# Seven block products for the gate, up and first feed-forward matrices of a four-layer model

## The chip, the cores and the metric

The kernel runs on one core of a Trainium2 chip. The metric is the device time of one execution in microseconds; lower is better. Data lie in SBUF (128 partitions); TensorE multiplies into PSUM banks, VectorE, ScalarE and GpSimd work on the rest, and the DMA queues of SyncE bring the weights from HBM. In the profile they are PE (with PEld for its weight loads), DVE, ACT, POOL and SP.

## The reference, cut to what matters

512 tokens of width 1024 go through four layers, in float32. The first two end in a gated feed-forward block of inner width 2816, the last two in a squared-ReLU block of inner width 4096.

```python
def swiglu(h, wg, wu, wd):
    return (jax.nn.silu(h @ wg) * (h @ wu)) @ wd

def sq_relu_mlp(x, w_up, w_down):
    return jnp.square(jax.nn.relu(x @ w_up)) @ w_down

# first block, layers 0 and 1
    h = h + mix                      # hybrid mixer, then convolution
    h = h + swiglu(rms_norm(h, ffn_norm[layer]), wg, wu, wd)
# second block, layers 0 and 1
    x = x + rmsnorm(m, norm_mixer_post[i])      # m: attention, then short convolution
    h = rmsnorm(x, norm_mlp_pre[i])
    x = x + rmsnorm(sq_relu_mlp(h, mlp_w_up[i], mlp_w_down[i]), norm_mlp_post[i])
```

## The kernel before, in words

**Layout.** Activations are kept transposed: eight tiles `res[0..7]` of 128 channels x 512 tokens hold the residual in float32. A normalised copy lies in `xh` (high part, fp32r) and `xl` (the rest, fp32r). Scratch tiles of 128x512 come from two lists, `rslots` (fp32r) and `fslots` (float32), oldest first.

**Matrix products.** Each weight block is loaded as float32 (`wraw`, 2048 columns, three buffers) and split by `load_w` (L218) in two halves of 1024: ScalarE rounds to `wh` (the helper's line is L101 for everything that ScalarE does), VectorE subtracts to `wl` (L235); `wh` and `wl` have two buffers of 2048 each. `mm3` (L239) then makes three matmuls for each output tile and k, `wh*xh` (L240), `wh*xl` (L241) and `wl*xh` (L242), each 128x128 by 512 tokens. `group` (L246) does this for four outputs of 128 rows and eight k: two loads of four k, 96 matmuls, four PSUM banks, after which `evac` takes each output. The tag `mm` has four banks and `at` four.

**Norms.** Only the gain is put in before a product (`split_x`, L332: ScalarE writes `xh`, VectorE `xl` at L334). The tokens' scale `rb` is made beside it by `bc_rstd`: `sumsq` squares the eight residual tiles on ScalarE, sums five on GpSimd (L316) and three on VectorE, and two matmuls with a matrix of ones (L326) give the sum over the channels to all partitions. `rb` is then multiplied into each output when it is taken.

**The gated block** `swiglu` (L606) has three parts of 8, 8 and 6 row tiles. A group computes two gate tiles and two up tiles: gate tiles are scaled (L621), put through SiLU on ScalarE and scaled again on GpSimd (L623), up tiles are multiplied by them (L625) and split (L339) to `hh`, `hl`. After each part `out_proj` multiplies by the second matrix and adds to the residual.

**The other block** `mlp` has four parts of two groups of four tiles each. `evac` scales (L1010), squares the ReLU (L1011) and splits (L339). The second matrix's outputs are added up in `post.m`; class `Post` squares and sums them (L791, GpSimd adds), makes their scale for each half of 256 tokens (L818), and `apply` multiplies (L810), adds to the residual (L811) and splits for the next product. The first groups of a block take their first load in halves of 256 tokens (`halves`), so that they can begin on the first half.

**What sets the order.** The program is written in the order of the data; the framework's scheduler puts every engine's instructions in a fixed row, and each engine works in that order. Tiles in the lists and pools come free when their last reader is done.

## Time and profile before

| | |
|---|---|
| time, median of 3 runs | 2519.17 us (2518.61 to 2525.0) |
| the profiled execution | 2523.11 us |
| its span in the trace | 2521.1 us |
| mean granted TensorE clock, share of full speed | 0.982 |
| PE busy, share of the span | 97% |
| DVE busy | 49% |
| ACT busy | 36% |
| POOL busy | 10% |
| read from HBM | 202.61 MB |

A matmul's end is modelled, so that a busy time adds up overlaps; the distance from one start to the next is what one costs in a row of them. A timeline row gives the start in us, its length, engine, line, operation, output and inputs, shape and count; a bracket behind it gives the engine's idle time ahead of the row and what ended it. A count above 1 joins equal neighbours.

### The profile page before, as it was taken

Reading aid. Unit: us, or ns where it says so; the run is one execution under the profiler, and the core shown is the slowest. Engines: PE = TensorE matmul, PEld = TensorE weight load, DVE = VectorE, ACT = ScalarE, POOL = GpSimd, SP = SyncE. Lnnn points to the kernel's source line nnn. Section 1 sums busy time; section 2 is a strip of 40 time slices with the busy share of each in tenths; the row PEclk is TensorE's granted clock in tenths of the full one; section 3 lists DMA queues with packets and bytes.
Section 4 is the critical chain, followed back from the end, with each engine's and each line's share of the span. In section 5 each row is a group of like instructions: output and inputs, shape, how many; then the busy total and the mean of one; then the engine's idle time right before and its main releaser. Section 6 shows DMA issues by size and latency. Waiting matters only on the chain.

```text
span 2521.1 us, 26712 instructions
## 1 busy us (share of the span) xinstructions
PE 2447.7 (97%) x10910; PEld 1940.4 (77%) x10910; DVE 1236.3 (49%) x1674; ACT 900.6 (36%) x1546; POOL 242.7 (10%) x223
## 2 busy tenths in 40 slices
PE   8999999999998799999999998999998999999997
PEld 6677788888786578888887677788887887788886
DVE  4333543333599744333345765443446544533454
ACT  4663432222664333222244455322224224322222
POOL 0000010100103111010100004000004103000002
PEclk9999999999999899999999999999999999999998
DMA  5112222322311132232232112233232222222320
GB/s 171 34 51 77 74 93 91 100 86 91 97 46 55 33 97 94 91 100 86 82 101 67 53 49 68 85 100 100 84 100 67 93 92 84 84 89 95 101 84 34
DMA packets 148075, 206.42 MB, mean 82 GB/s; under 512 B 5822, under 2 KB 88305, under 8 KB 147953
## 3 DMA queue, kind: packets, MB, share of 16 engines
q1 hardware_dynamic: 147921, 204.72, 25.3%
q8 instruction: 85, 1.39, 0.2%
q14 instruction: 37, 0.30, 0.0%
q10 hardware_dynamic: 32, 0.01, 0.0%
HBM read 202.61 MB, written 2.10 MB: 81 GB/s over the span
## 4 chain that ended last, share of the span: by engine, by line
PE 61%; DVE 3%; POOL 2%; ACT 2%; issue 1%; ACTq 0%; POOLq 0%; DVEq 0%
PE ps L242 18%; PE ps L240 18%; PE ps L241 18%; DVE fs L717 1%; ACT fs L101 1%; PE ps L912 1%; POOL fs L811 1%; PE ps L948 1%; POOL fs L316 1%; PE ps L285 1%; PE ps L284 1%; PE ps L283 1%; DVE fs L810 0%; POOL fs L791 0%; PE ps L940 0%
## 5 line engine op out<-in xcount | busy, mean ns | idle before, releaser
L240 PE MATMUL ps<-rs,wh 128*128 128x512 f32 (+1 forms) x3008 | 1176.2, 391 | 12.7 <-ACT rs L101 8.9
L241 PE MATMUL ps<-rs,wh 128*128 128x512 f32 (+1 forms) x3008 | 1173.2, 390 | 4.0 <-DVE rs L334 4.0
L242 PE MATMUL ps<-rs,wl 128*128 128x512 f32 (+1 forms) x3008 | 1171.7, 390 | 2.4 <-DVE wl L235 2.4
L235 DVE TENSOR_TENSOR wl<-wraw,wh 128x1024 fp32r<-128x1024 f32 (+2 forms) x386 | 459.5, 1219 | 711.7 <-ACT wh L101 706.9
L101 ACT ACTIVATE wh<-wraw 128x1024 fp32r<-128x1024 f32 (+2 forms) x386 | 385.3, 1039 | 890.3 <-PE ps L241 612.7
L240 PEld LDWEIGHTS ps<-rs,wh 128*128 128x128 f32 x3008 | 570.1, 190 | 146.6 <-ACT rs L101 11.3
L241 PEld LDWEIGHTS ps<-rs,wh 128*128 128x128 f32 x3008 | 570.8, 190 | 136.0 <-DVE rs L334 5.4
L242 PEld LDWEIGHTS ps<-rs,wl 128*128 128x128 f32 x3008 | 570.3, 190 | 131.0 <-DVE wl L235 2.9
L101 ACT ACTIVATE fs<-fs 128x512 f32<-128x512 f32 (+2 forms) x289 | 154.4, 549 | 174.6 <-DVE fs L621 93.7
L101 ACT ACTIVATE rs<-fs 128x512 fp32r<-128x512 f32 x160 | 97.6, 616 | 189.6 <-DVE fs L1011 112.2
L339 DVE TENSOR_TENSOR rs<-fs,rs 128x512 fp32r<-128x512 f32 x136 | 93.8, 696 | 51.1 <-ACT rs L101 51.0
L791 POOL TENSOR_TENSOR fs<-fs,fs 128x256 f32<-128x256 f32 (+1 forms) x44 | 46.1, 1047 | 753.6 <-ACT fs L101 752.7
L623 POOL TENSOR_TENSOR fs<-fs,fs 128x512 f32<-128x512 f32 x44 | 56.6, 1288 | 621.1 <-ACT fs L101 594.3
L717 DVE SCALAR_TENSOR_TENSOR fs<-fs,vec,fs 128x497 f32<-128x497 f32 (+15 forms) x139 | 98.0, 778 | 0.0
L101 ACT ACTIVATE fs<-ps 128x512 f32<-128x512 f32 (+1 forms) x99 | 50.8, 524 | 69.2 <-PE ps L242 30.7
L706 PE MATMUL ps<-rs,rs 128*128 128x500 f32 (+13 forms) x279 | 67.8, 397 | 7.9 <-ACT rs L101 7.9
L316 POOL TENSOR_TENSOR fs<-fs,fs 128x512 f32<-128x512 f32 x28 | 46.9, 1676 | 278.8 <-ACT fs L101 277.7
L706 PEld LDWEIGHTS ps<-rs,rs 128*128 128x128 f32 x279 | 53.8, 193 | 21.2 <-ACT rs L101 9.8
L101 ACT ACTIVATE rs<-fs,vec 128x512 fp32r<-128x512 f32 (+1 forms) x76 | 48.2, 651 | 60.5 <-DVE fs L811 15.9
L334 DVE SCALAR_TENSOR_TENSOR rs<-fs,vec,rs 128x512 fp32r<-128x512 f32 (+1 forms) x76 | 60.4, 829 | 7.3 <-ACT rs L101 7.1
L283 PE MATMUL ps<-wh,rs 128*128 128x512 f32 (+1 forms) x160 | 62.2, 391 | 0.0
L284 PE MATMUL ps<-wl,rs 128*128 128x512 f32 (+1 forms) x160 | 61.9, 387 | 0.0
(201 smaller groups left out, 1456.9 us busy)
## 6 DMA issues: line engine op xcount, KB each, us to landing
wraw<-in_mlp_w_up_dram SPq DMA_DIRECT2D x32, 1024.0 KB
wraw<-in_mlp_w_down_dram SPq DMA_DIRECT2D x32, 1024.0 KB
wraw<-in_ffn_w_gate_dram SPq DMA_DIRECT2D x44, 512.0 KB
wraw<-in_ffn_w_up_dram SPq DMA_DIRECT2D x44, 512.0 KB
wraw<-in_ffn_w_down_dram SPq DMA_DIRECT2D x20, 1024.0 KB
wraw<-in_cv_w_pw_dram SPq DMA_DIRECT2D x16, 512.0 KB
wraw<-in_attn_w_qkv_dram SPq DMA_DIRECT2D x16, 512.0 KB
wraw<-in_conv_w_in_dram SPq DMA_DIRECT2D x16, 512.0 KB
```

The source lines that it names most:

```text
L101: r = self.engine.activation(out, in_, func, **kw)
L235: dve.tensor_sub(wl[:, s], raw[:, s], b(wh[:, s]))
L240: pe.matmul(ps, wh, h, start=start, stop=False, skip_group_check=True)
L241: pe.matmul(ps, wh, l, start=False, stop=False, skip_group_check=True)
L242: pe.matmul(ps, wl, h, start=False, stop=stop, skip_group_check=True)
L283: pe.matmul(ps, hs[kk + k][:, ts_], wh[:, k, :], start=ci == 0 and k == 0, stop=False)
L284: pe.matmul(ps, hs[kk + k][:, ts_], wl[:, k, :], start=False, stop=False)
L316: r = eng.tensor_add(acc, acc, s)
L334: dve.scalar_tensor_tensor(xl[k][:, x], res[k][:, x], gain, b(xh[k][:, x]), ALU.mult, ALU.subtract)
L339: dve.tensor_sub(l, src, b(h))
L706: pe.matmul(pc[:, s:], d, x[:, : T - s], start=i == 0, stop=i == len(todo) - 1, skip_group_check=True)
L717: dve.scalar_tensor_tensor(x[:, s:], u[:, : T - s], wdv(s, ct), x[:, s:], ALU.mult, ALU.add)
```

## The change

Both first matrices are multiplied in quarters. For a group of four row tiles, the weights (1024 channels x 512 rows) and the normalised tokens (1024 channels x 512 tokens) are cut into 2x2 blocks, and the four output blocks (256 rows x 256 tokens) are made of seven block products instead of eight (the Winograd form of Strassen's scheme). Each product is 4 k x 2 row tiles x 3 = 24 matmuls with 256 tokens, into one PSUM bank.

- `group_s` replaces `group`. It loads the weights into the same two `wraw` buffers, makes sums of weight blocks in place on VectorE, splits seven 1024-wide parts (`w_parts`: four buffers each of `wh` and `wl`, 1024 wide), and adds the products up on VectorE. `evac(n, th, ps)` gets row-tile pair `n` and token half `th`, two row tiles beside each other.
- The sums of token blocks are made once for a block, when the residual is ready: `xh`, `xl` of channels 0 to 511 hold the first half of the tokens and a difference of the halves; three further combinations lie in `so[0]` (high) and `so[1]` (rest). `split_s` and `split_s_half` take the place of `split_x` there.
- In `swiglu` the up tiles come first: they keep no scale; the gate tiles are scaled and put through SiLU; the tokens' scale of the up tiles is multiplied in after the second matrix (`down_evac`). GpSimd's L623 goes. In `mlp` nothing is scaled behind the first matrix; ScalarE does ReLU and square; `rb` squared is multiplied in after the second (`evac_last`).
- Constants, the stage of the vectors, five float tiles and the rounded constants move to pools that live for one phase (`Phase`), so that `so` finds room.

```diff
-NF = 34
+NF = 29
+NX = 5
...
-    rslots = [cpool.tile([P, T], F32R, name=f"rs{i}") for i in range(32)]
+    pairs = [cpool.tile([P, 2, T], F32R, name=f"rs{i}") for i in range(16)]
+    rslots = [p[:, h, :] for p in pairs for h in range(2)]
...
+    def w_parts(src, n):
+        wh = wpool.tile([P, 1024], F32R, tag="wh", name=f"wh{n_p[0]}", bufs=4)
+        wl = wpool.tile([P, 1024], F32R, tag="wl", name=f"wl{n_p[0]}", bufs=4)
...
+        act.activation(v(wh), src, AF.Copy)
+        dve.tensor_sub(v(wl), src, v(b(wh)))
+        return wh, wl
...
-        wh = wpool.tile([P, 2048], F32R, tag="wh", name=f"wh{i}", bufs=2)
-        wl = wpool.tile([P, 2048], F32R, tag="wl", name=f"wl{i}", bufs=2)
...
+    def open_s():
+        ph = Phase(0)
+        for i in range(2):
+            so[i] = ph.tile([P, 4, 3, 256], F32R, f"so{i}")
+        return ph
+
+    def split_s3(k, gain):
+        d = F()
+        dve.tensor_sub(d[:, :256], res[k][:, T0], res[k][:, T1])
+        act.activation(xh[k][:, T1], d[:, :256], AF.Copy, scale=gain)
+        dve.scalar_tensor_tensor(xl[k][:, T1], d[:, :256], gain, b(xh[k][:, T1]), ALU.mult, ALU.subtract)
+        freeF(d)
+
+    def split_sums(k, gain1, gain2):
+        s, s4 = F(2)
+        act.activation(s4[:, T0], res[4 + k][:, T1], AF.Copy, scale=gain2)
+        dve.scalar_tensor_tensor(s[:, T0], res[k][:, T1], gain1, s4[:, T0], ALU.mult, ALU.add)
+        dve.scalar_tensor_tensor(s[:, T1], res[k][:, T0], gain1, s[:, T0], ALU.mult, ALU.subtract)
+        dve.scalar_tensor_tensor(s4[:, T1], res[4 + k][:, T0], gain2, s[:, T1], ALU.mult, ALU.add)
+        for src, n0, n in ((s, 0, 2), (s4[:, T1], 2, 1)):
+            h, l = (t[:, k, n0 : n0 + n, :].rearrange("p n t -> p (n t)") for t in so)
+            split_to(h, l, src)
+        freeF(s, s4)
...
+    def split_s_half(k, gname, gi, i):
+
+        g = V(gname, gi * 8 + k)
+        if i == 0 or k >= 4:
+            split_x(k, g, HALVES[i])
+        if i == 1:
+            if k < 4:
+                split_s3(k, g)
+            else:
+                split_sums(k - 4, V(gname, gi * 8 + k - 4), g)
+
+    def group_s(w0, w1, evac, first=False):
...
+        def product(ps, w, x, start=False):
+            for k in range(4):
+                for p in range(2):
+                    wh, wl = (t[:, k * 256 + p * P : k * 256 + (p + 1) * P] for t in w)
+                    mm3(ps[:, p * 256 : (p + 1) * 256], wh, wl, *x(k), start and k == 0 and p == 0, k == 3)
...
+        a, d, g = bank(), bank("at"), bank("at")
+        o11 = parts(b11)
+        dve.tensor_sub(b11, b12, b11)
+        product(a, o11, xs(0, T0), True)
+        p1 = F()
+        act.activation(p1, a, AF.Copy)
+
+
+        if first:
+            product(d, parts(b21), xs(4, T0), True)
+        product(g, parts(b11), sums(0), True)
+        p5 = F()
+        act.activation(p5, g, AF.Copy)
+        o22 = parts(b22)
+        dve.tensor_sub(b12, b22, b12)
+        dve.tensor_sub(b22, b11, b22)
+        product(a, parts(b22), sums(1))
+        u2 = F()
+        act.activation(u2, a, AF.Copy)
+        product(g, o22, sums(2))
+        dve.tensor_add(u2, g, u2)
+        evac(1, 0, u2)
+        product(a, parts(b12), xs(0, T1))
+        dve.tensor_add(p5, a, p5)
+        evac(1, 1, p5)
+        if not first:
+            product(d, parts(b21), xs(4, T0), True)
+        dve.tensor_add(p1, d, p1)
+        evac(0, 0, p1)
+        dve.tensor_add(b21, b21, b22)
+        product(a, parts(b21), xs(4, T1))
+        evac(0, 1, a)
...
+                def evac(n, th, ps):
+                    x = HALVES[th]
+                    if n == 1:
+                        dve.tensor_mul(halves_2(ps), halves_2(ps), rb[:, x].unsqueeze(1).to_broadcast([P, 2, 256]))
+                        act.activation(ps, ps, AF.Silu)
+                        ss[th] = ps
+                        return
+                    dve.tensor_mul(ss[th], ps, ss[th])
+                    split_to(ph[fc][:, :, x], pl[fc][:, :, x], halves_2(ss[th]))
...
+            def down_evac(o, ps, tr):
+                s = F()
+                dve.tensor_mul(s, ps, rb)
+                if pi < len(parts) - 1:
+                    pool_e.tensor_add(res[o], res[o], s)
+                else:
+                    dve.tensor_add(res[o], res[o], s)
+                    split_x(o, V(nxt[0], nxt[1] * 8 + o))
+                freeF(s)
...
+                dve.tensor_mul(self.m[o][:, x], self.m[o][:, x], scale[:, x])
...
-            for k in range(4 if nxt else 8):
+            for k in range(4 if nxt and not self.sums else 8):
                 self.apply(k, tr)
...
+                def evac(n, th, ps):
+                    s = F() if (n, th) == (0, 1) else ps
+                    act.activation(s, ps, AF.Relu)
+                    act.activation(s, s, AF.Square)
+                    split_to(ph[g * 2 + n][:, :, HALVES[th]], pl[g * 2 + n][:, :, HALVES[th]], halves_2(s))
...
```

How the rows of the engines stand differs at three places. Lines of the changed kernel: L273 splits weights (`w_parts`), L480, L492, L493 and L507 are the sums of weight blocks, L498, L501 and L505 the sums of products in `group_s`, L796 and L800 scale and gate in `swiglu`, L396 splits outputs (`split_to`).

VectorE, in the first gated block, where one group follows another, before:

```order
L621 TENSOR_TENSOR fs32_129<-ps120_2306,fs16_113 128x512
L621 TENSOR_TENSOR fs8_105<-ps121_2307,fs16_113 128x512
L625 TENSOR_TENSOR fs32_129<-ps122_2308,fs32_129 128x512
L339 TENSOR_TENSOR rs29_94<-fs32_129,rs28_93 128x512
L625 TENSOR_TENSOR fs8_105<-ps123_2309,fs8_105 128x512
L235 TENSOR_TENSOR wl25_2499<-wraw25_2497,wh25_2498 128x1024 x2
L339 TENSOR_TENSOR rs27_92<-fs8_105,rs26_91 128x512
L235 TENSOR_TENSOR wl26_2572<-wraw26_2570,wh26_2571 128x1024 x2
```

and in the changed kernel, from the end of one group's weights (wl48) to the next group's third split (wl51):

```order
L273 TENSOR_TENSOR wl48_2536<-wraw21_2344,wh48_2535 128x1024
L498 TENSOR_TENSOR fs26_107<-ps117_2349,fs26_107 128x512
L273 TENSOR_TENSOR wl49_2576<-wraw22_2566,wh49_2575 128x1024
L796 TENSOR_TENSOR fs26_107<-fs26_107,fs18_99 128x512
L480 TENSOR_TENSOR wraw22_2566<-wraw22_2566 128x4x256
L501 TENSOR_TENSOR fs17_98<-ps115_2347,fs17_98 128x512
L492 TENSOR_TENSOR wraw22_2566<-wraw23_2569,wraw22_2566 128x4x256
L796 TENSOR_TENSOR fs17_98<-fs17_98,fs18_99 128x512
L505 TENSOR_TENSOR fs23_104<-ps116_2348,fs23_104 128x512
L273 TENSOR_TENSOR wl50_2606<-wraw22_2566,wh50_2605 128x1024
L800 TENSOR_TENSOR fs26_107<-fs23_104,fs26_107 128x512
L273 TENSOR_TENSOR wl51_2635<-wraw23_2569,wh51_2634 128x1024
```

Splits and sums of the next group's weights now stand between the additions of this group's products.

TensorE, at the first group of the third layer's feed-forward block: `ps434` is the bank of the sum of squares, `ps435` to `ps438` are the group's outputs. Before:

```order
L240 MATMUL ps438_9903<-rs3_68,wh114_9905 128x256
L241 MATMUL ps438_9903<-rs11_76,wh114_9905 128x256
L242 MATMUL ps438_9903<-rs3_68,wl114_9906 128x256
L326 MATMUL ps434_9895<-fs25_122,ones_133 128x512
L240 MATMUL ps435_9900<-rs4_69,wh115_10009 128x512
L241 MATMUL ps435_9900<-rs12_77,wh115_10009 128x512
```

and in the changed kernel, where `ps411` is the second half's sum of squares of the mixer's output, `ps412` that of the residual, `ps413` the first product and `ps414` the second:

```order
L297 MATMUL ps413_12348<-rs1_66,wh293_12351 128x256
L298 MATMUL ps413_12348<-rs5_70,wh293_12351 128x256
L299 MATMUL ps413_12348<-rs1_66,wl293_12352 128x256
L1016 MATMUL ps411_12252<-fs12_93,ones_121 128x256
L383 MATMUL ps412_12338<-fs21_102,ones_121 128x512
L297 MATMUL ps414_12349<-rs2_67,wh294_12381 128x256
L298 MATMUL ps414_12349<-rs6_71,wh294_12381 128x256
L299 MATMUL ps414_12349<-rs2_67,wl294_12382 128x256
```

The residual's sum of squares (L326, now L383) stood behind 96 matmuls of the group; now it stands behind the first product and ahead of the second.

VectorE at the same place, before:

```order
L810 SCALAR_TENSOR_TENSOR fs30_127<-fs30_127,vec_137,fs14_111 128x512
L810 SCALAR_TENSOR_TENSOR fs32_129<-fs32_129,vec_137,fs14_111 128x512
L811 TENSOR_TENSOR fs4_101<-fs4_101,fs30_127 128x512
L811 TENSOR_TENSOR fs5_102<-fs5_102,fs32_129 128x512
L810 SCALAR_TENSOR_TENSOR fs13_110<-fs13_110,vec_137,fs14_111 128x512
L334 SCALAR_TENSOR_TENSOR rs12_77<-fs4_101,vec_137,rs4_69 128x512
```

and in the changed kernel (L1006 and L1007 answer to L810 and L811, L391 to L334; L415 and L417 are `split_s3`, L423 to L425 the sums in `split_sums`):

```order
L1006 SCALAR_TENSOR_TENSOR fs25_106<-fs25_106,vec_125,fs28_109 128x256
L415 TENSOR_TENSOR fs18_99<-fs3_84 128x256
L1007 TENSOR_TENSOR fs4_85<-fs4_85,fs23_104 128x256
L1007 TENSOR_TENSOR fs5_86<-fs5_86,fs25_106 128x256
L417 SCALAR_TENSOR_TENSOR rs5_70<-fs18_99,vec_125,rs1_66 128x256
L391 SCALAR_TENSOR_TENSOR rs6_71<-fs4_85,vec_125,rs2_67 128x256
L423 SCALAR_TENSOR_TENSOR fs26_107<-fs0_81,vec_125,fs16_97 128x256
L391 SCALAR_TENSOR_TENSOR rs6_71<-fs5_86,vec_125,rs2_67 128x256
L424 SCALAR_TENSOR_TENSOR fs26_107<-fs0_81,vec_125,fs26_107 128x256
L423 SCALAR_TENSOR_TENSOR fs11_92<-fs1_82,vec_125,fs15_96 128x256
L425 SCALAR_TENSOR_TENSOR fs16_97<-fs4_85,vec_125,fs26_107 128x256
```

The sums of token blocks stand between the last splits, and all tiles are taken in halves of 256.

## Rows read from the trace of the kernel before

**Rows 1.** The page: busy us, share, count; costliest groups (busy, mean ns, idle).
```profile
PE 2447.7 (97%) x10910; PEld 1940.4 (77%) x10910; DVE 1236.3 (49%) x1674; ACT 900.6 (36%) x1546; POOL 242.7 (10%) x223
...
L623 POOL TENSOR_TENSOR fs<-fs,fs 128x512 f32<-128x512 f32 x44 | 56.6, 1288 | 621.1 <-ACT fs L101 594.3
```

**Rows 2.** Two windows: busy us (count) of PE, PEld, DVE, ACT, POOL; clock; DMA.
```profile
450.00:500.00 50.00, 50.00 (x216) 40.09 (x215) 20.34 (x23) 15.17 (x19) 5.83 (x5) 1.00 0.28 86
1700.00:1750.00 50.00, 50.00 (x216) 40.25 (x215) 19.63 (x22) 11.15 (x12) 0.00 (x0) 1.00 0.27 84
```

**Rows 3.** Timeline of PE in the second window: start, length, work.
```profile
1699.83 0.40 PE L242 MATMUL ps<-rs,wl 128*128 128x512 f32 x1
...
1704.96 0.40 PE L240 MATMUL ps<-rs,wh 128*128 128x512 f32 x1
```

**Rows 4.** Timeline of PE, 256-wide matmuls at the attention output's end.
```profile
1537.71 0.28 PE L240 MATMUL ps<-rs,wh 128*128 128x256 f32 x1
...
1544.18 0.28 PE L240 MATMUL ps<-rs,wh 128*128 128x256 f32 x1
...
1545.94 0.28 PE L240 MATMUL ps<-rs,wh 128*128 128x256 f32 x1
...
1550.18 0.28 PE L240 MATMUL ps<-rs,wh 128*128 128x256 f32 x1
```

**Rows 5.** Timeline of DVE inside the gated and the other feed-forward blocks.
```profile
518.00 2.36 DVE L235 TENSOR_TENSOR wl<-wraw,wh 128x1024 fp32r<-128x1024 f32 x2 [8.24 <-ACT wh L101]
520.28 0.68 DVE L621 TENSOR_TENSOR fs<-ps,fs 128x512 f32<-128x512 f32 x1
...
1770.22 0.68 DVE L1011 SCALAR_TENSOR_TENSOR fs<-fs 128x512 f32<-128x512 f32 x1
1770.82 1.22 DVE L235 TENSOR_TENSOR wl<-wraw,wh 128x1024 fp32r<-128x1024 f32 x1
...
1782.55 0.68 DVE L1010 TENSOR_TENSOR fs<-ps,fs 128x512 f32<-128x512 f32 x1
1783.27 0.69 DVE L1011 SCALAR_TENSOR_TENSOR fs<-fs 128x512 f32<-128x512 f32 x1
```

**Rows 6.** Timeline of ACT: weight splits in a row, then one alone.
```profile
505.71 2.01 ACT L101 ACTIVATE wh<-wraw 128x1024 fp32r<-128x1024 f32 x2 [1.19 <-PE ps L241]
507.63 0.62 ACT L101 ACTIVATE rs<-fs 128x512 fp32r<-128x512 f32 x1
...
1554.26 1.05 ACT L101 ACTIVATE wh<-wraw 128x1024 fp32r<-128x1024 f32 x1
```

**Rows 7.** Timeline of DVE at the second gated block's start.
```profile
902.34 0.75 DVE L769 SCALAR_TENSOR_TENSOR fs<-ps,vec,fs 128x512 f32<-128x512 f32 x1
...
910.36 0.74 DVE L769 SCALAR_TENSOR_TENSOR fs<-ps,vec,fs 128x512 f32<-128x512 f32 x1
```

**Rows 8.** Timeline of PE at the same place.
```profile
910.15 1.02 PE L326 MATMUL ps<-fs,ones 128*128 128x512 f32 x2
```

**Rows 9.** Timeline of POOL at the third layer's feed-forward start.
```profile
1565.08 8.12 POOL L316 TENSOR_TENSOR fs<-fs,fs 128x512 f32<-128x512 f32 x4 [1.66 <-ACT fs L101]
```

**Rows 10.** Timeline of PE at that start.
```profile
1573.25 2.07 PE L326 MATMUL ps<-fs,ones 128*128 128x512 f32 x2 [4.98 <-POOL fs L316]
...
1575.97 0.63 PE L242 MATMUL ps<-rs,wl 128*128 128x512 f32 x1
1576.40 0.63 PE L240 MATMUL ps<-rs,wh 128*128 128x512 f32 x1
```

**Rows 11.** Timeline of DVE at that start.
```profile
1559.34 2.63 DVE L810 SCALAR_TENSOR_TENSOR fs<-fs,vec,fs 128x256 f32<-128x256 f32 x4 [2.77 <-ACT fs L101]
...
1566.94 1.78 DVE L810 SCALAR_TENSOR_TENSOR fs<-fs,vec,fs 128x512 f32<-128x512 f32 x1
...
1573.67 0.74 DVE L810 SCALAR_TENSOR_TENSOR fs<-fs,vec,fs 128x512 f32<-128x512 f32 x1
...
1589.37 1.28 DVE L1010 TENSOR_TENSOR fs<-ps,fs 128x512 f32<-128x512 f32 x2
```

More of the change, by code (lines that the diff above doesn't have):

```diff
@@ L143, in freeF, with RP, __init__, tile @@
             fslots.extend(t if isinstance(t, list) else [t])
+    def RP(n):
+        free = {id(t) for t in rslots}
+        ix = sorted((i for i in range(16) if all(id(t) in free for t in halves_of[i])),
+                    key=lambda i: next(n for n, t in enumerate(rslots) if t is halves_of[i][0]))[:n]
+        assert len(ix) == n
+        ts = [t for i in ix for t in halves_of[i]]
+        gone = {id(t) for t in ts}
+        rslots[:] = [t for t in rslots if id(t) not in gone]
+        return [pairs[i] for i in ix], ts
+    n_ph = [0]
+    class Phase:
+        def __init__(self, nx):
+            n_ph[0] += 1
+            self.name = f"ph{n_ph[0]}"
+            self.cm = tc.tile_pool(name=self.name, bufs=1, reuse_waits="tile")
+            self.pool = self.cm.__enter__()
+            self.xs = [self.tile([P, T], F32, f"fx{i}") for i in range(nx)]
+            fslots.extend(self.xs)
+        def tile(self, shape, dtype, name):
+            return self.pool.tile(shape, dtype, name=f"{self.name}_{name}")
+        def close(self):
+            mine = {id(t) for t in self.xs}
+            assert sum(id(t) in mine for t in fslots) == len(self.xs)
+            fslots[:] = [t for t in fslots if id(t) not in mine]
+            self.cm.__exit__(None, None, None)
+    phase = Phase(NX)
     res = F(8)
@@ L148, in body, with const_tiles @@
     b = lambda t: t.bitcast(F32)
-    NC = const_array().shape[1]
-    cst = cpool.tile([P, NC], F32, name="cst")
-    C = {n: cst[:, o : o + w] for n, (o, w, _) in _consts().items()}
-    ident = C["ident"]
+    ident = cpool.tile([P, P], F32, name="ident")
+    C = {"ident": ident}
+    def const_tiles(names):
+        lo = _consts()[names[0]][0]
+        hi = sum(_consts()[names[-1]][:2])
+        t = phase.tile([P, hi - lo], F32, "cst")
+        for n in names:
+            o, w, _ = _consts()[n]
+            C[n] = t[:, o - lo : o - lo + w]
+        return t, consts[:, lo:hi]
+    mix_cst = const_tiles(["ntri", "sbmask", "gtri", "bones", "gind"])
     sync.dma_start(ident, consts[:, :P])
@@ L189, in body @@
     ]
-    stage = cpool.tile([P, 5 * P], F32, name="stage")
+    stage = phase.tile([P, 5 * P], F32, "stage")
     v_off = [0]
@@ new lines, in group_s @@
+    def group_s(w0, w1, evac, first=False):
+        bb = []
+        for kh in range(2):
+            n_w[0] += 1
+            raw = wpool.tile([P, 2048], F32, tag="wraw", name=f"wraw{n_w[0]}", bufs=3)
+            rv = raw[:, :].rearrange("p (k c) -> p k c", k=4)
+            rows = slice(kh * 512, (kh + 1) * 512)
+            if w0[0] is w1[0] and w1[1] == w0[1] + 256:
+                sync.dma_start(rv, w0[0][rows, w0[1] : w0[1] + 512].rearrange("(k p) c -> p k c", p=P))
+            else:
+                for n, (ap, c) in enumerate((w0, w1)):
+                    sync.dma_start(rv[:, :, n * 256 : (n + 1) * 256], ap[rows, c : c + 256].rearrange("(k p) c -> p k c", p=P))
+            bb += [rv[:, :, :256], rv[:, :, 256:]]
+        b11, b12, b21, b22 = bb
+        def product(ps, w, x, start=False):
[3 more added lines that the diff above has]
+                    mm3(ps[:, p * 256 : (p + 1) * 256], wh, wl, *x(k), start and k == 0 and p == 0, k == 3)
+        xs = lambda k0, tr: lambda k: (xh[k0 + k][:, tr], xl[k0 + k][:, tr])
+        sums = lambda n: lambda k: (so[0][:, k, n, :], so[1][:, k, n, :])
+        parts = lambda t: w_parts(t, 1024)
+        a, d, g = bank(), bank("at"), bank("at")
[28 more added lines that the diff above has]
+        evac(0, 1, a)
@@ L799, in evac_last, with then @@
                 dve.tensor_add(self.m[o][:, x], self.m[o][:, x], ps[:, x])
+                dve.tensor_mul(self.m[o][:, x], self.m[o][:, x], scale[:, x])
             self.squares(o, tr)
-        def then(self, gname, gi, nxt, each=None):
+        def then(self, gname, gi, nxt, each=None, sums=False):
+            self.sums = sums
             self.args = (gname, gi, nxt, each)
@@ L811, in apply @@
             (pool_e if k < 4 else dve).tensor_add(res[k][:, x], res[k][:, x], m[:, x])
-            if nxt:
+            if nxt and self.sums:
+                split_s_half(k, nxt[0], nxt[1], HALVES.index(x))
+            elif nxt:
                 split_x(k, V(nxt[0], nxt[1] * 8 + k), x)
@@ L826, in finish @@
         def finish(self):
-            if self.args[2]:
+            if self.args[2] and not self.sums:
                 for k in range(4, 8):
@@ L991, in body @@
         freeF(v)
-    post = Post().then("mpost", 0, ("fpre", 0))
-    out_proj(A["attn_w_o_2"][0], 0, 8, oh, ol, lambda o, ps, tr: post.evac_last(o, ps, tr, True), k_outer=True, halves=True,
+    phase.close()
+    phase = open_s()
+    post = Post().then("mpost", 0, ("fpre", 0), sums=True)
+    out_proj(A["attn_w_o_2"][0], 0, 8, oh, ol, lambda o, ps, tr: post.evac_last(o, ps, tr), k_outer=True, halves=True,
              after_half=post.half)
@@ L1065, in body @@
     freeF(rb, rb2)
-    post = Post().then("mpost", 1, ("fpre", 1))
-    out_proj(A["conv_w_out_2"][0], 0, 8, hh, hl, lambda o, ps, tr: post.evac_last(o, ps, tr, True), halves=True,
+    post = Post().then("mpost", 1, ("fpre", 1), sums=True)
+    out_proj(A["conv_w_out_2"][0], 0, 8, hh, hl, lambda o, ps, tr: post.evac_last(o, ps, tr), halves=True,
              after_half=post.half)
```

113 lines of the change are left out of this document (66 added, 47 removed).

## The prediction, made before the changed kernel ran

> **What bounds the kernel now.** I read the page first, then the stretches, then single rows. The page: TensorE is busy 97% of the span, VectorE 49%, ScalarE 36% [rows 1]; two quiet stretches, one in each part that the change touches, show it 50.00 of 50 us busy at a granted clock of 1.00, with VectorE at 20 us and ScalarE at 11 to 15 [rows 2]. There is nothing to fill in there: only fewer or cheaper matmuls help. What a matmul costs is read from starts, since the modelled durations overlap: 22 steps from 1699.83 to 1704.96 give **233 ns for a 512-wide one** [rows 3]. A 256-wide one of the same kind starts every **113.5 ns** (57 steps, 1537.71 to 1544.18) or **117.8 ns** (36 steps, 1545.94 to 1550.18) [rows 4], so halving the width costs nothing by itself; I take 115.7.
>
> **Part 1, the matmuls.** A gate/up group, like a group of the first feed-forward matrix, has 4 outputs x 8 k x 3 = 96 matmuls of 512: 96 x 0.233 = 22.4 us. Seven products of 24 matmuls of 256 are 168 x 0.1157 = 19.4 us (19.1 to 19.8 by the two paces), 2.78 us a product. There are 22 such groups in the gated layers (two layers of 4, 4 and 3) and 16 in the others (two layers, four pairs). If nothing else mattered: 38 x 3.0 = 114 us. The rule that speaks against it: the Trainium skill (TensorE: Matmul & The Clock Gate, "Back-to-back issue gap") has streams of weight load and matmul at about 81 ns for 128 columns and 131 for 512, far from proportional. An estimate from that page, put between the two, would be some 0.74 of the 512 pace. The trace disagrees: 113.5 to 117.8 is half.
>
> **Part 2, what VectorE and ScalarE get.** A group now splits seven 1024-wide weight parts instead of four and makes four 1024-wide sums of weight blocks. Back to back, VectorE takes 1.14 us for 1024 (518.00 to 520.28 is two) and 0.60 for 512; if an instruction needs the one ahead of it, 0.72 [rows 5]. ScalarE takes 0.96 for a part in a row, 1.05 alone, 0.62 for 512 [rows 6]. VectorE per group: 11 x 1.14 + 9 x 0.60 = 17.9 us in the gated layers (three sums of products, two scalings, two gatings, two splits), 11 x 1.14 + 7 x 0.60 = 16.7 in the others. Below 19.4, but its queue is in order and waits for TensorE, and four buffers for split parts tie the two. I followed the queues through one group.
>
> *The last product* may write its bank only when VectorE has read it (L501). From the end of product 4: ScalarE splits the last weights (1.1, its buffer is free only now), VectorE completes the split (1.2), L498 (0.6), the next group's first split (1.14), an evacuation (0.6), L480 (1.14), L501 (0.65): 6.4 us. TensorE needs 2 x 2.78 = 5.6. So every group loses 0.9 us: **20.3 instead of 22.4, a gain of 2.1**.
>
> *In the gated layers* the queue goes on (the order fence ends at the third split): L492, scaling, L505, split, gating, split, L396, L800, L493, then ScalarE's and VectorE's part of the third product's weights. That is eight of 1024 (9.2), eight of 512 (4.8) and two ScalarE splits (2.2), 16.3 us from the end of product 4; product 3 needs the low part after its first two matmuls, so add 2.55 for it and 2.78 for product 4: a loop of **21.6 us, a gain of 0.8** wherever a group follows a group. After a down projection VectorE has caught up, and the 2.1 holds.
>
> Sum of the loops: gated layers 6 x 2.1 + 16 x 0.8 = 25; others, without each layer's first group, 14 x 2.1 = 29.
>
> **Part 3, the starts.** The block sums of the tokens need both halves of the residual. At a gated layer the last projection hands over a tile every 2.7 us (four from 902.34 to 910.36 [rows 7]), and TensorE shows no idle at 910.15, where the sum of squares (L326) begins [rows 8]. A tile of 4 to 7 now costs VectorE 0.75 + 0.75 + three 256-wide at 0.5 + 0.6 + 0.4 = 4.0 us, with weights and sums of weights 22 us from 902.3, against two products and the end of the projection on TensorE (14 us): the first product on the sums waits some 3 us, the weights of the one after come late, and the next group inherits it. I put 4.7 us per start, from the 2.1 that this group then doesn't gain, 0.5 lost and 2.1 in the next (0 to 9): 25 - 9 = 16.
>
> At a feed-forward start both orders show the difference: the sum of squares (L383) now stands *ahead* of the product on the second half of the channels; before (L326) it stood behind 96 matmuls. It needs the whole residual, and GpSimd's four adds, 8.12 us [rows 9]. Before, TensorE waits 4.98 us there, then paces 0.43 per matmul of 512, which is its 1.2 GHz level [rows 10], and the group's last outputs are taken at 1589.4 [rows 11]. After: the second half's scale is ready near 1560.7 (before 1559.3 [rows 11]; the first half's pass over the residual now has eight tiles instead of four ahead of it, which I put at 1.4); VectorE then has 28 multiply-adds of 256 (0.655 each beside GpSimd [rows 11], taken 0.5), 12 of 256 at 0.4 and 8 others of 0.6 to 1.2: 25 us, to 1586. GpSimd's adds end near 1577, TensorE idle for some 18 us until then; the first product on the sums ends near 1588.8, four more (11.1) make 1599.9. **10.5 us later than before**, twice: -21. The bounds: 5 (all at 0.4) and 20 (all at 0.655 and a start at half clock). The sharing is seen in rows: the same multiply-add of 512 takes 1.78 beside GpSimd's adds and 0.74 after them [rows 11]. The Trainium skill (SBUF — State Buffer, "SBUF: two separate sides") calls the sharing an exclusive lock for a whole instruction; by it, each of four adds holds up one VectorE instruction by about 1 us, 4 us per start. The trace agrees, and 2 of the 10.5 are for that; taking all of it would move the sum by 4.
>
> **Part 4, small things.** The tokens' scale behind the second matrix adds a 0.4 us multiply per half to the two feed-forward ends, on the path, and a 0.6 one to each tile of the gated ends, where TensorE has the next group's first tiles to work on: 3 us together (0 to 8). GpSimd's gating multiplies (1288 ns x 44 [rows 1]) go; in a stretch where TensorE has no idle [rows 2] that frees nothing. The pools move tiles; their loads stand where they stood, so 0, between -3 and 3: the cover is the value projection.
>
> **The sum:** 16 + 29 - 21 - 3 = 21 us off the profiled execution's 2523.1 (span 2521.1 and 2.0 around it): 2502. The median of the runs is 3.9 below that execution, so **2498**.
>
> **Rivals.**
> *TensorE stays the bound* (the evacuations find gaps that I did not give them): groups at 19.1 to 19.8, 2.6 to 3.3 x 34 = 88 to 112, less 24 at starts and ends: 64 to 88, 2431 to 2455 by the median. For it: 17.9 of 19.4 us. Against: the buffer that is free only after product 4.
> *Slower: VectorE's queue costs more than back to back.* One mechanism: each of its instructions costs its busy time (1.22 and 0.69 [rows 5]), since ahead of most stands a wait. Some 0.09 more on 16 instructions in 16 loops (23), on six in 20 (11), on 40 at four starts (14): 48 us, and 27 slower, 2546. It decides from 0.04 us per instruction on. Against: most neighbours in the new order don't need each other; for: 0.72 where they do.
> *No change:* half of that, 2512 to 2527.
> *The products don't keep the pace.* They change weights every matmul and half a bank every three; at 133 ns a start (22.4 / 168) the gain is zero before any wait: 2540 with the 21 of the starts. [rows 4] show 113 to 118 in another order. By the page's estimate the pace would be 0.74 x 0.233 = 0.172, a group 29 us, 38 x 6.6 = 250 slower, near 2770: 1%, since [rows 4] contradict it.
>
> **Chances.** Forecast (2482 to 2511) 0.43; TensorE bound 0.19; no change 0.16; slower queue 0.19; pace 0.03. The range takes in most of the second and of the slower one: 2442 to 2540. Faster by over 0.3% (7.5 us, about what a measurement tells from no change) 0.62, within 0.16, slower 0.22.
>
> **What would show it.** Right: 256-wide starts at 113 to 118 ns within products; a gap of about 1 us ahead of the seventh product, released by VectorE; in gated layers a second ahead of the third; groups near 20.3 and 21.6; a long wait at L383, released by GpSimd, at two places, and the half clock behind it. Wrong: groups at 19.4 (the loops are no loops), above 22.4 (the slower rival), no wait at L383, or time lost in the attention or convolution stretches, which I left alone.

## The result and the profile after

The changed kernel takes **2487.99 us** (median of 4 runs, 2484.07 to 2490.03) where the kernel before takes 2519.09: the ratio is **0.9869, with a 95% interval of 0.9849 to 0.9889**. That is 31 us faster, 10 us better than the forecast of 2498 and inside its range of 2442 to 2540. The profiled execution took 2486.35 us, its span is 2484.5.

The page of the changed kernel, first its busy times (us, share of the span, count), then the group of VectorE's weight splits:

```profile
PE 2362.6 (95%) x13550; PEld 2008.3 (81%) x13550; DVE 1620.5 (65%) x2096; ACT 1186.9 (48%) x1966; POOL 233.7 (9%) x212
...
L273 DVE TENSOR_TENSOR wl<-wraw,wh 128x1024 fp32r<-128x1024 f32 x500 | 606.7, 1221 | 513.3 <-ACT wh L102 512.5
```

Beside [rows 1]: TensorE gives up 85 us of its busy time, VectorE takes on 384. The two quiet stretches of [rows 2] now read as follows (windows: busy us and count of PE, PEld, DVE, ACT, POOL, then clock and DMA):

```profile
450.00:500.00 50.00, 49.77 (x419) 49.36 (x418) 46.19 (x52) 27.37 (x34) 0.00 (x0) 1.00 0.35 106
1640.00:1670.00 30.00, 30.00 (x256) 30.00 (x255) 25.35 (x26) 22.74 (x33) 0.00 (x0) 1.00 0.43 141
```

In the gated block VectorE went from 20.3 to 46.2 of 50 us and TensorE loses only 0.23; in the other block VectorE works 25.35 of 30 (16.8 us in the 19.9 of a group; the prediction had 16.7).

Where the time went, by stretches. Each border is the start or end of a run of TensorE's matmuls that both traces have; the convolution stands with the first gated block, since no such border lies between the two:

| stretch, us | before | after | difference |
|---|---|---|---|
| up to the first gated block | 301.7 | 301.9 | +0.2 |
| first gated block and convolution | 608.2 | 592.5 | -15.7 |
| second gated block | 371.6 | 353.8 | -17.8 |
| attention | 256.2 | 255.9 | -0.3 |
| third layer's feed-forward | 375.9 | 372.1 | -3.8 |
| its end and the short convolution | 197.2 | 199.1 | +1.9 |
| fourth layer's feed-forward | 376.0 | 372.3 | -3.7 |
| its end | 34.2 | 37.1 | +2.9 |
| span | 2521.1 | 2484.5 | -36.6 |

The traces differ by 36.6, the medians by 31.1: the profiled execution of before lies 4.0 over its median and that of after 1.6 under its own. Stretches that no edit touches also move from one trace to the next (the first one ended between 300.3 and 305.3 in the traces of this study), so a stretch is read to some 2 us.

**A group.** TensorE's timeline in the changed kernel gives it (start, length, work). In the gated block from one group's first product to the next, with the wait in the third product, and in the other block:

```profile
458.72 0.28 PE L297 MATMUL ps<-rs,wh 128*128 128x256 f32 x1
...
464.53 0.28 PE L298 MATMUL ps<-ph_so,wh 128*128 128x256 f32 x1
464.95 0.39 PE L299 MATMUL ps<-ph_so,wl 128*128 128x256 f32 x1
...
476.09 0.28 PE L299 MATMUL ps<-rs,wl 128*128 128x256 f32 x1
476.21 0.28 PE L297 MATMUL ps<-rs,wh 128*128 128x256 f32 x1
...
479.02 0.28 PE L297 MATMUL ps<-rs,wh 128*128 128x256 f32 x1
...
1632.95 0.28 PE L297 MATMUL ps<-rs,wh 128*128 128x256 f32 x1
...
1652.85 0.28 PE L297 MATMUL ps<-rs,wh 128*128 128x256 f32 x1
```

Gated groups take 20.30 here (20.17 in the mean of four, the first of which doesn't wait), the others **19.90**, where 96 matmuls of 512 took 22.4. 19.90 is 168 matmuls at 118.5 ns: products on `xh` step at 117, those on the sums `so` at 120. The seventh product (476.21) follows the sixth without a gap; the third waits 0.3 for its low part (464.53 to 464.95).

**A start.** At the third layer's feed-forward block TensorE shows this:

```profile
1525.33 1.22 PE L1016 MATMUL ps<-fs,ones 128*128 128x256 f32 x2 [4.69 <-POOL fs L984]
1544.71 2.08 PE L383 MATMUL ps<-fs,ones 128*128 128x512 f32 x2 [18.16 <-POOL fs L373]
1545.80 1.20 PE L297 MATMUL ps<-rs,wh 128*128 128x256 f32 x1
1546.80 0.41 PE L298 MATMUL ps<-rs,wh 128*128 128x256 f32 x1
```

and GpSimd this:

```profile
1541.87 2.79 POOL L373 TENSOR_TENSOR fs<-fs,fs 128x512 f32<-128x512 f32 x2 [1.75 <-ACT fs L102]
```

VectorE, beside these adds of GpSimd and a little later without them:

```profile
1542.05 1.48 DVE L425 SCALAR_TENSOR_TENSOR fs<-fs,vec,fs 128x256 f32<-128x256 f32 x1
1543.46 1.48 DVE L1007 TENSOR_TENSOR fs<-fs,fs 128x256 f32<-128x256 f32 x1
...
1547.38 0.41 DVE L1007 TENSOR_TENSOR fs<-fs,fs 128x256 f32<-128x256 f32 x1
1547.72 0.47 DVE L425 SCALAR_TENSOR_TENSOR fs<-fs,vec,fs 128x256 f32<-128x256 f32 x1
```

The last 512-wide matmul of the attention's output and the first one of the second matrix, in the changed kernel and before:

```profile
1503.73 0.40 PE L299 MATMUL ps<-rs,wl 128*128 128x512 f32 x1
...
1587.98 0.39 PE L297 MATMUL ps<-rs,wh 128*128 128x512 f32 x1
```

```profile
1537.48 0.40 PE L242 MATMUL ps<-rs,wl 128*128 128x512 f32 x1
...
1611.16 0.40 PE L240 MATMUL ps<-rs,wh 128*128 128x512 f32 x1
```

From start to start these are 84.3 us, before 73.7. The fourth layer's start reads the same within 0.3 us.

### The profile page after: what moved, and what is told of

Same layout as the page of the kernel before. It is cut to its first block, busy times and chain, and to the rows that moved or that the text cites. A ratio compares the mean times of both kernels' runs of the same rounds, so it can differ in the third digit from the quotient of the medians.

```text
span 2484.5 us, 33155 instructions
## 1 busy us (share of the span) xinstructions
PE 2362.6 (95%) x13550; PEld 2008.3 (81%) x13550; DVE 1620.5 (65%) x2096; ACT 1186.9 (48%) x1966; POOL 233.7 (9%) x212
## 5 line engine op out<-in xcount | busy, mean ns | idle before, releaser
L297 PE MATMUL ps<-rs,wh 128*128 128x512 f32 (+1 forms) x2976 | 1028.9, 346 | 9.1 <-ACT rs L102 8.2
L298 PE MATMUL ps<-rs,wh 128*128 128x512 f32 (+1 forms) x2976 | 1028.8, 346 | 5.4 <-DVE rs L391 5.4
L299 PE MATMUL ps<-rs,wl 128*128 128x512 f32 (+1 forms) x2976 | 1024.5, 344 | 2.4 <-DVE wl L273 2.4
L273 DVE TENSOR_TENSOR wl<-wraw,wh 128x1024 fp32r<-128x1024 f32 x500 | 606.7, 1221 | 513.3 <-ACT wh L102 512.5
L102 ACT ACTIVATE wh<-wraw 128x1024 fp32r<-128x1024 f32 x500 | 519.7, 1047 | 682.7 <-PE ps L298 553.0
L297 PE MATMUL ps<-ph_so,wh 128*128 128x256 f32 x912 | 260.0, 285 | 5.0 <-ACT fs L102 3.4
L299 PE MATMUL ps<-ph_so,wl 128*128 128x256 f32 x912 | 259.5, 285 | 3.6 <-DVE wl L273 2.4
L298 PE MATMUL ps<-ph_so,wh 128*128 128x256 f32 x912 | 258.6, 284 | 0.7 <-DVE ph_so L396 0.7
L297 PEld LDWEIGHTS ps<-ph_so,wh 128*128 128x128 f32 x912 | 175.1, 192 | 7.5 <-ACT fs L102 4.8
L299 PEld LDWEIGHTS ps<-ph_so,wl 128*128 128x128 f32 x912 | 174.9, 192 | 7.7 <-DVE wl L273 7.5
L102 ACT ACTIVATE fs<-ps 128x512 f32<-128x512 f32 (+1 forms) x207 | 116.3, 564 | 129.2 <-PE ps L299 100.5
L298 PEld LDWEIGHTS ps<-ph_so,wh 128*128 128x128 f32 x912 | 175.2, 192 | 1.7 <-DVE ph_so L396 0.9
L102 ACT ACTIVATE rs<-fs 128x512 fp32r<-128x512 f32 (+1 forms) x148 | 91.7, 623 | 78.5 <-DVE fs L800 44.1
L396 DVE TENSOR_TENSOR rs<-fs,rs 128x512 fp32r<-128x512 f32 x133 | 91.0, 689 | 19.2 <-ACT rs L102 18.8
```

The lines of the kernel that those rows point to most:

```text
L102: r = self.engine.activation(out, in_, func, **kw)
L273: dve.tensor_sub(v(wl), src, v(b(wh)))
L297: pe.matmul(ps, wh, h, start=start, stop=False, skip_group_check=True)
L298: pe.matmul(ps, wh, l, start=False, stop=False, skip_group_check=True)
L299: pe.matmul(ps, wl, h, start=False, stop=stop, skip_group_check=True)
L396: dve.tensor_sub(l, src, b(h))
```

## The experiments

Each edit is against the changed kernel unless said otherwise. Times stand against the kernel before on the same chip, as ratio and difference of medians.

**One half of the products at a time, and none.** In e1 `mlp` calls `group` again, in e2 `swiglu` does, in e3 both; the token sums of that block go with it.

```diff
-                group_s((wu, f0 * P), (wu, f0 * P + 256), evac, pi == 0 and g == 0)
+                group(k_chunks([(wu, f0 * P, (f0 + 4) * P)], 0, 8), FOUR, xh, xl, evac, pi == 0 and g == 0, h0)
...
-                group_s((wu, col), (wg, col), evac, pi == 0 and fc == 0)
+                group(k_chunks([(wg, col, col + 256), (wu, col, col + 256)], 0, 8), FOUR, xh, xl, evac, pi == 0 and fc == 0)
```

> The third and fourth layers' feed-forward blocks go back to 96 matmuls of 512 a group with whole tiles of tokens (their scale stays behind the second matrix); the gated blocks keep the seven products. Theory from the trace after: the two gated stretches alone gave 15.8 and 17.8 us, the ends of the other blocks cost 1.9 and 2.9: 2519.1 - 33.6 + 4.8 = 2490, within 3. By the shares of the forecast (16 for the gated blocks, 3 lost at ends): 2506. Between the two lies the question whether the gated loop of 21.6 us per group exists; the trace after shows groups at 20.2.

> The opposite half: gated blocks with 96 matmuls of 512 a group (scale still behind the second matrix), the other two with seven products. Theory: the two blocks gain 3.8 and 3.7 us net of their starts and lose 4.8 at their ends: 2516, within 3. If the long wait at each start (18 us of TensorE idle in the trace after) weighs more than the groups give back, over 2522.

> No block products at all: what is left of the change is the scale behind the second matrix, the buffers of 1024 and the pools by phase. Theory: only the two feed-forward ends get longer, 1.9 and 2.9 us: 2524, within 3. Forecast: 3 lost, 2522. If the moved scale frees VectorE and GpSimd to any use, below 2517.

Measured: e1 2495.18, ratio 0.9901 (0.9886 to 0.9916), -25.3 us; e2 2523.70, 1.0012 (1.0002 to 1.0021), +3.3; e3 2531.86, **1.0047 (1.0030 to 1.0063), +11.4**. The gated blocks' products are worth 36.7 us (e3 to e1), the others' 8.2 (e3 to e2), together 44.9; with +11.4 they make -33.5, and the changed kernel has -31.1: the parts add. e1 came 5 over its expectation, e2 and e3 7 to 8. One reason is shown by e3: what is left of the change without any product costs 11 us, not 4.8 or the 3 of the forecast. Another is that the expectations took stretches from two traces that differ by 36.6 us where the medians differ by 31.1; how much falls to each was not separated.

**Where the 11 us are: addresses.** Through the whole trace of e3 the 512-wide matmuls step at 234.3 ns instead of the 233.4 of before. Two rows, 36 steps apart, in e3:

```profile
1699.93 0.39 PE L299 MATMUL ps<-rs,wl 128*128 128x512 f32 x1
...
1708.36 0.40 PE L299 MATMUL ps<-rs,wl 128*128 128x512 f32 x1
```

8.43 / 36 = 234.2 ns. The matmuls themselves are the same. What is different in the built program is where the split weights start: before, 64 bytes behind a multiple of 128 in each partition; in the changed kernel, 96 behind one, because other small tiles ahead of them went to the phase pools. Two kernels try this, with one unused tile:

```diff
     ones = cpool.tile([P, P], F32, name="ones")
+    cpool.tile([P, 8], F32, name="pad")
```

> The changed kernel with one unused tile of 32 bytes per partition in the constant pool, so that the split weights and the token sums start at addresses that are multiples of 128 (the changed kernel has them 96 behind one, the kernel before 64). Reason: in the trace of e3, which has no block products, each 512-wide matmul takes 234.3 ns instead of 233.4 of the kernel before, some 8 us over all of them. Theory A, the start address costs some ns per matmul: 512-wide back to 233.4 or less (4 us), 256-wide from 117 to 120 down to 113 to 117 (6400 x 3 = 19 us, of which VectorE's row in the gated groups may keep a third): 2466 to 2480. Theory B, the pace comes from the smaller tiles or the pairs: no change, 2488.

> The kernel before with the same unused 32 bytes in the constant pool and nothing else: its split weights now start 96 behind a multiple of 128, as in the changed kernel. Theory A: each 512-wide matmul 0.9 ns longer, 8 us in all, 2528. Theory B: 2520.

Measured: e5 2483.37, ratio **0.9841 (0.9828 to 0.9855)**, where the changed kernel has 0.9869 (0.9849 to 0.9889): 7 us faster by the ratios, whose intervals just overlap, and 4.6 by the medians. e6, the kernel *before* with 32 bytes more and no other edit, 2529.91, **1.0028 (1.0017 to 1.0038)**: 7 us slower. The same 36 steps in e5 (8.36 us, 232.2 ns) and in e6 (8.43, 234.2):

```profile
1690.05 0.39 PE L299 MATMUL ps<-rs,wh 128*128 128x512 f32 x1
...
1698.41 0.39 PE L299 MATMUL ps<-rs,wh 128*128 128x512 f32 x1
```

```profile
1699.99 0.39 PE L242 MATMUL ps<-rs,wh 128*128 128x512 f32 x1
...
1708.42 0.40 PE L242 MATMUL ps<-rs,wh 128*128 128x512 f32 x1
```

Over all 512-wide matmuls of a trace the mean step is 232.6 ns with the weights at a multiple of 128 (e5), 233.4 at 64 behind (before), 234.3 at 96 behind (after, e3, e6). Theory A holds for these. Its second half fell: the 256-wide ones don't get faster, a group of the third layer takes 20.02 in e5 instead of 19.90 (119 and 120 ns). So e5 gains only on the 4,600 wide ones, 4,600 x 1.7 = 8 us, and gives back 0.12 x 16 in groups.

Yet the 256-wide ones answer to the address too. The 57 steps of the attention's output that take 113.5 ns each before [rows 4] take 6.70 / 57 = 117.5 in e6:

```profile
1542.29 0.28 PE L241 MATMUL ps<-rs,wh 128*128 128x256 f32 x1
...
1548.99 0.28 PE L241 MATMUL ps<-rs,wh 128*128 128x256 f32 x1
```

Over all 256-wide matmuls outside the products the mean step is 115.8 ns at 64 behind (before), 118.0 at 96 behind (e6) and 119.1 at a multiple (e12): their best of the three offsets is the one that the change left.

> The kernel of e3 (no block products) with the 32 unused bytes. e3 is 11 us slower than the kernel before. Theory: 8 of these are the address (234.3 against 233.4 ns, 8200 matmuls) and some 4 the longer ends; at 232.5 ns, as in e5, it should take 15 us less than e3: 2517. If the 11 us are something else, such as the moved scale and pools: 2532.

e12 is e3 with the pad: 2519.85, ratio 0.9995 (0.9984 to 1.0006), 12 us under e3. So the 11 us of e3 are 7 to 8 of addresses, and the rest is spent at the ends: in e3's trace the stretch behind the third layer's block is 1.8 longer than before and the last one 3.3. Only the last repeats in e12 (2.9, against 0.2 for the other).

**The start of the other blocks.** e4 asks for the residual's sum of squares after the first part's second matrix.

```diff
-        rb, acc = bc_rstd(res)
-        freeF(acc)
-
-        dve.tensor_mul(rb, rb, rb)
         post = Post().then("fpost", layer, nxt, each)
...
             freeR(hh, hl)
+            if pi == 0:
+                rb, acc = bc_rstd(res)
+                freeF(acc)
+                dve.tensor_mul(rb, rb, rb)
```

> The changed kernel, but in the third and fourth layer's feed-forward blocks the residual's sum of squares is asked for after the first part's second matrix, where its result is still early enough. Theory A: the 18.2 us of idle ahead of L383 and the half clock behind it are the sum's, GpSimd's adds and what they cost VectorE: the second product (2.8 us) runs in the wait, VectorE is rid of two adds and of sharing, 6 to 10 us a start, 2468 to 2476 in all. Theory B: VectorE's row of token sums, busy without a break from 1520 to 1552, holds the third product by itself: only the second product moves, 2 to 4 us a start, 2480 to 2484. No gain (2488) if the sum costs as much where it is put.

Measured: 2488.94, ratio 0.9878 (0.9863 to 0.9893): no gain. TensorE's waits at the same start:

```profile
1527.39 1.22 PE L1016 MATMUL ps<-fs,ones 128*128 128x256 f32 x2 [4.70 <-POOL fs L984]
1539.94 0.58 PE L297 MATMUL ps<-ph_so,wh 128*128 128x256 f32 x1 [6.60 <-ACT ph_so L102]
1543.19 0.58 PE L297 MATMUL ps<-ph_so,wh 128*128 128x256 f32 x1 [1.08 <-ACT ph_so L102]
...
1553.27 0.58 PE L297 MATMUL ps<-ph_so,wh 128*128 128x256 f32 x1 [3.93 <-ACT ph_so L102]
1554.75 0.58 PE L298 MATMUL ps<-ph_so,wh 128*128 128x256 f32 x1 [0.89 <-DVE ph_so L396]
```

The 18.16 are gone, and the products on the sums wait instead, k by k, for each token sum; the last comes at 1554.75. Windows of the changed kernel and of e4 tell why:

```profile
1520.00:1550.00 30.00, 7.15 (x36) 5.20 (x35) 29.53 (x54) 17.30 (x38) 10.85 (x10) 0.60 0.00 1
```

```profile
1530.00:1555.00 25.00, 10.22 (x38) 7.96 (x38) 25.00 (x49) 12.32 (x25) 6.50 (x6) 0.57 0.02 2
1554.75:1559.60 4.85, 4.85 (x22) 4.85 (x23) 3.24 (x4) 3.92 (x6) 0.00 (x0) 0.50 0.70 215
```

VectorE is busy 29.53 of 30 and 25.00 of 25 us. The wait was shown as GpSimd's, and GpSimd did release it, but behind it stood VectorE's row of some 50 instructions; no run made this row shorter by itself. TensorE was busy 7.15 of 30 and 10.22 of 25 us there, and the granted clock was 0.60 and 0.57. Behind its last wait e4 goes on at 0.50 for 4.85 us, with a 256-wide matmul every 0.21 us, where the changed kernel steps at 0.12 from 1547.6 on: some 2 us of the 2.8 that the second product had won. The starts of e4 are 0.5 and 1.6 us shorter. Theory B holds, without even its small gain: the later sum took that back (the second matrix behind it takes 46.3 us instead of 45.0, and each of the two groups after that 20.16 instead of 19.90).

**VectorE's round trip in a group.** e7 gives the split weights five buffers (and takes three float tiles from the phases with token sums), e8 adds two idle instructions of 1024 a group.

```diff
-        wh = wpool.tile([P, 1024], F32R, tag="wh", name=f"wh{n_p[0]}", bufs=4)
-        wl = wpool.tile([P, 1024], F32R, tag="wl", name=f"wl{n_p[0]}", bufs=4)
+        wh = wpool.tile([P, 1024], F32R, tag="wh", name=f"wh{n_p[0]}", bufs=5)
+        wl = wpool.tile([P, 1024], F32R, tag="wl", name=f"wl{n_p[0]}", bufs=5)
...
         dve.tensor_sub(b11, b12, b11)
+        dve.scalar_tensor_tensor(b21, b21, 1.0, b21, ALU.mult, ALU.max)
+        dve.scalar_tensor_tensor(b21, b21, 1.0, b21, ALU.mult, ALU.max)
```

> The changed kernel with five buffers of split weights instead of four (high and low), room made by keeping three float tiles out of the phases that hold the token sums. Theory: what the third product of a gated group waits for (0.33 us in the trace after) is VectorE's row, not a buffer; but with one buffer more the splits of the next group are done before the sums of products, so the row shifts: the wait goes, 16 x 0.33 = 5 us, 2483. Rival: the row as a whole is late, 2488.

> The changed kernel with two more 1024-wide VectorE instructions per group that leave the data as they are (some 2.3 us a group), behind the first sum of weight blocks. The rival 'VectorE's queue costs more than back to back' priced 1.4 us a group at 48. Theory: gated groups have no slack left (the third product waits already), 16 x 2.3 = 37 us; the other blocks' groups have some: of 19.9 us VectorE works 16.7, so their 14 lose 0 to 1 us each: 2525 to 2540. If the groups were bound by TensorE alone: 2488 to 2495.

e7: 2489.79, ratio 0.9872 (0.9855 to 0.9889), no gain in all, but the parts moved. A gated group of e7 takes TensorE's own 19.90:

```profile
433.98 0.28 PE L297 MATMUL ps<-rs,wh 128*128 128x256 f32 x1
...
453.88 0.28 PE L297 MATMUL ps<-rs,wh 128*128 128x256 f32 x1
```

and the second gated block 349.2 us instead of 353.8, while the other two blocks went from 372.1 and 372.3 to 376.0 and 376.6, all of it at their starts. That the three missing float tiles do this is only argued. e8: 2530.62, ratio **1.0036 (1.0022 to 1.0049)**, 42 us over the changed kernel. Four gated groups of e8, from the first product to the second matrix, and the windows of these four in the changed kernel and in e8:

```profile
444.67 0.28 PE L297 MATMUL ps<-rs,wh 128*128 128x256 f32 x1
...
531.33 0.40 PE L297 MATMUL ps<-rs,wh 128*128 128x512 f32 x1
```

```profile
438.82:519.49 80.67, 80.35 (x673) 79.75 (x672) 71.41 (x78) 44.64 (x55) 2.15 (x1) 1.00 0.36 111
```

```profile
444.67:531.33 86.66, 81.70 (x674) 80.13 (x673) 77.58 (x83) 43.20 (x54) 2.14 (x1) 1.00 0.32 103
```

That is 21.66 a group, 1.5 more for 2.3 us of VectorE work (two of 1.14), and VectorE's share is nearly the same: 71.41 of 80.67 us (89%), in e8 77.58 of 86.66 (90%); a tenth of its time is idle in both. So the loop is a round trip, TensorE frees a buffer, ScalarE and VectorE fill it in their rows, and not VectorE's capacity: buffers shorten it (e7), work in the row lengthens it (e8). The other blocks' groups went from 19.90 to 20.6. 22 x 1.5 + 16 x 0.7 = 44 us is all of the loss.

**Towards a better kernel.** All three have the pad of e5. e9 has five buffers for the high parts alone and one float tile less in the phases with token sums; e10 asks for the gated blocks' sum of squares behind the third product of their first group; e11 does both.

```diff
         product(a, parts(b22), sums(1))
+        if mid:
+            mid()
```

> The kernel of e5 with five buffers for the high parts of the split weights (four for the low ones), paid for with one float tile in the phases that hold the token sums. Theory: in e7 the groups ran at TensorE's own 19.90 us in the gated blocks too, but the three missing float tiles made each start of the other blocks 4 us longer; one missing tile costs less, and ScalarE's split is the part that waits for a buffer: gated groups from 20.2 to 20.0, 22 x 0.2 = 4 us, starts of the gated blocks 3 us each as in e7, other starts 0 to 2 us longer: 2471 to 2481 where e5 has 2483. If the low parts' buffers are what counts: 2483.

> The kernel of e5 with the sum of squares of the two gated blocks asked for behind the third product of their first group, instead of ahead of the group. Theory: the first parts of the gated blocks take 91.3 and 88.3 us in the trace after where four groups at 20.17 would take 80.7; 4 us of the first is TensorE idle ahead of the sum's second matmul. Moving it lets the second and third products begin: 3 to 6 us in all, 2477 to 2481. Rival, as in e4: VectorE's row holds the products by itself, no gain, 2483.

> Both of the last two. If the gains add: 2468 to 2478; if both take the same wait away: as the better of the two.

e9: **2479.31, ratio 0.9829 (0.9814 to 0.9845)**, the lowest time of this study, 41 us under the kernel before and clear of the changed kernel (e5, e9 and e11 are not told apart by their intervals); a gated group takes 20.03 (20.06 in the mean), and the other blocks' 371.7 and 372.2 show no loss for one float tile:

```profile
440.35 0.28 PE L298 MATMUL ps<-rs,wh 128*128 128x256 f32 x1
...
460.38 0.28 PE L298 MATMUL ps<-rs,wh 128*128 128x256 f32 x1
```

e10: 2484.72, 0.9852 (0.9837 to 0.9868), and e11: 2480.07, 0.9830 (0.9815 to 0.9845): the moved sum brings nothing in either. In e5 TensorE waits 3.95 us for it at the first gated block's start; in e10 that wait is gone, and these stand there instead:

```profile
309.45 0.39 PE L298 MATMUL ps<-rs,wh 128*128 128x256 f32 x1 [0.88 <-ACT rs L102]
311.37 0.58 PE L299 MATMUL ps<-rs,wh 128*128 128x256 f32 x1 [1.53 <-DVE rs L392]
316.42 0.39 PE L300 MATMUL ps<-ph_so,wl 128*128 128x256 f32 x1 [1.08 <-DVE wl L274]
```

It is e4 again: a wait moves along a full row.

## Why the prediction was right, and where it was not

**Part 1, the matmuls: right, a little short.** Seven products cost less than eight, nearly in the ratio of their columns. The step is 118.5 ns, not 115.7: the faster half of [rows 4] doesn't come back, and products on `so` step at 120. A group without waits takes 19.90 where I had 19.4 (19.1 to 19.8). The paces of [rows 4] belonged to weights 64 bytes behind a multiple of 128; with the changed kernel's 96 behind, the kernel before loses the 113.5 as well (e6). If the products followed the two means there (115.8 and 118.0 ns), that is 0.4 of the 0.5 us; this is an estimate, since no run had the products at 64 behind.

**Part 2, the loops: the step that failed.** I let the seventh product wait 0.9 us and the gated loop take 21.6. VectorE's load was right (in the gated blocks 71.41 us for four groups, 17.9 each, as forecast; in the others 16.8 against 16.7), and so was the place of the second wait, but I gave the last weights of a group the buffer of the fourth product. They take that of the third, one product earlier. ScalarE in the changed kernel shows it, then VectorE:

```profile
468.52 1.06 ACT L102 ACTIVATE wh<-wraw 128x1024 fp32r<-128x1024 f32 x1
470.65 1.06 ACT L102 ACTIVATE wh<-wraw 128x1024 fp32r<-128x1024 f32 x1 [1.07 <-PE ps L298]
```

```profile
472.11 1.22 DVE L273 TENSOR_TENSOR wl<-wraw,wh 128x1024 fp32r<-128x1024 f32 x1
473.36 1.23 DVE L480 TENSOR_TENSOR wraw<-wraw 128x1024 f32<-128x1024 f32 x1
474.51 0.68 DVE L501 TENSOR_TENSOR fs<-ps,fs 128x512 f32<-128x512 f32 x1
```

At 468.52 the last weights are split while product 4 still runs; at 470.65 its buffer goes to the next group's first weights. From there L501 ends 4.6 us later (475.2), not 6.4, and the seventh product, due at 476.21, finds its bank free. The gated loop loses the same 2.2 us (a split on ScalarE and one on VectorE): 19.4 by that working, and 20.17 measured. Priced as a sum: 22 groups x 2.2 = 49 us where I had 25, and in the other blocks 14 x 2.5 = 35 where I had 29.

**Part 3, the starts: right in kind, too small.** The long wait at L383 came where it was forecast, released by GpSimd, 18.16 us against "some 18", with the half clock behind it (0.50 granted from 1545 to 1547). The first group ends 13.1 us later than before (84.3 - 73.7 = 10.6, plus the 2.5 that the second group gains) where I had 10.5 and bounds of 5 and 20. The part that I named second, VectorE's row, bounds it more than the sum of squares: without the sum there, e4 gains 0.5 and 1.6 us. Some 2 us of the shortfall stand in the rows: each of GpSimd's four adds holds up one VectorE instruction, 1.48 us where the same takes 0.41 to 0.47, 4 us a start where the 10.5 held 2. At the gated blocks the first part of four groups takes 91.3 and 88.3 us (302.56 to 393.85 for the first) where 4 x 20.17 is 80.7: 10.6 and 7.6 lost per start where I had 4.7, just over the upper bound of 9 for one of them. The two errors in the gated blocks pull against each other: 49 - 18 = 31 from groups and starts, and 33.5 in the stretches of the table, against a forecast of 16.

**Part 4, small things: mis-sized.** Ends 1.9 and 2.9 us, some 5 instead of 3, are within what I had allowed. But "The pools move tiles; their loads stand where they stood, so 0, between -3 and 3" was wrong: moving tiles moved the weights' addresses, 0.9 ns on each 512-wide matmul, 4 us here and 8 in e3, and the pace of the 256-wide ones with them (part 1).

**The rivals.** *TensorE stays the bound* is nearest to what happens within groups (19.90, and 20.17 with a last 0.3 us of waiting); its time of 2431 to 2455 fails on the starts and the step. *Slower by VectorE's row* is a real mechanism, and the gated groups have no reserve against it: e8 adds 2.3 us of work a group and ends slower than the kernel before. *The products don't keep the pace* is out: 0.117 to 0.120 against 0.133 from which the gain would vanish. By the Trainium skill (TensorE: Matmul & The Clock Gate, "Back-to-back issue gap"), the estimate had been 0.74 of the 512 pace for half the columns; the trace gives 118.5 / 234.3 = 0.51, and the measurement decides.

Of the forecast of 21 us, then, the other blocks came as said (8 forecast, 7.5 measured, both terms larger), the gated blocks were 17.5 better and the rest 2 worse; the medians show 31. That the number came so near is in part luck: the groups gave back some 84 us where I had 54, the starts took 44 (18 and 26) where I had 30, and these two errors partly cancel.

## To carry to other kernels

Before pricing a loop through buffers, look up which buffer each transfer really takes: one place earlier or later made 2 us a group in the working above, more than the gain in question. When a long wait names an engine, look at which other engine is busy without a break in that window: here moving the named work (e4, e10) only moved the wait. And when tiles move between pools, compare the step of untouched matmuls before and after, for each width: here a changed start address showed in it, and a pad of 32 bytes took it back for the wide ones.
